# A mean over 8,192 rows: two pairs folded at double width, another engine for one group, and a last piece of one block stored as one row

## The chip, the cores and the metric

The kernel runs on one core of one Trainium2 chip. The metric is the device time of one execution in microseconds (us), and the profile's span, first to last instruction, is some 2 us shorter.

## The reference

```
x = randn(8192, 8192) in fp32
out = mean(x, axis=0)          # 8192 values
```

The input is 268 MB and the output 32 KB. Each input byte is used once.

## The kernel before

The rows form 64 groups of 128, one row for each partition. `bufs` holds six rows of 8,192 columns per partition. Rows 0 to 3 are two buffers, each for a pair of groups (8.39 MB, 64 KB per partition). Row 4 is `both`, a scratch row, and row 5 is `acc`. VectorE folds each pair into `both` and then adds that to `acc`. SyncE issues all loads, each of which waits until VectorE has read the buffer that it overwrites.

```python
add(bufs[:, 2:4, :], bufs[:, 2:4, :], bufs[:, 0:2, :], [first])
add(bufs[:, 4:6, :], bufs[:, 4:6, :], bufs[:, 2:4, :], [second])
add(acc, acc, both, [])
tc.keep_in_program_order(nc.scalar.copy(out=warm[:], in_=ones[:]))
g = 6
while g < G - 10:
    u = (g + 2) % 4
    dma = load_rows(g, u, 2)
    add(both, bufs[:, u, :], bufs[:, u + 1, :], [dma])   # the pair's buffer is free after this
    add(acc, acc, both, [])
    g += 2
# ... single groups 54 to 61 ...
load(r62, rows(g))
tc.keep_in_program_order(nc.gpsimd.tensor_add(
    out=acc[:, 13 * F:], in0=acc[:, 13 * F:], in1=r62[:, 13 * F:]))
g += 1
for lo, hi in [(0, 8), (12, 14), (14, 16)]:              # F = 512 columns
    load(r63[:, lo * F:hi * F], rows(g)[:, lo * F:hi * F])
```

The sum over partitions is made by TensorE with a matrix of 1/M. Each block of columns goes to a group of 32 rows of a PSUM bank, so that a result lies on partitions 0, 32, 64 and 96 and is stored from these four. The end of the kernel copies the banks to SBUF and stores them:

```python
copy(tails[0], ends[0][:])                                # ScalarE
nc.vector.tensor_copy(out=tails[1], in_=ends[1][:])
landed(...)                                               # SyncE waits for earlier loads
s01 = store(nc.sync, ..., res[0:P:32, 0:2, :])            # first eight blocks
s3 = store(nc.scalar, *end(0))                            # blocks 12 and 13
store(nc.sync, *end(1))                                   # blocks 14 and 15, the last piece
landed(loads[-2], s2)
landed(loads[-1], adds[-1])
landed(s01, s3)
```

## Time and profile before

| | before |
|---|---|
| time, median of 3 | 628.64 us (628.49 to 628.82) |
| profiled span | 626.7 us |
| last load lands | 623.02 us |
| from there to the end of the span | 3.69 us |
| share of the DMA engines, 2 to 622 us | 1.00 |

The prediction below shows the page, the stretches and the end of the chain. I call **lead** the time from a load's issue to the landing of the load ahead of it in the queue. While the lead is long, the DMA engines have the next load's work before they finish the last one's. These are the issues of two of the loads in SyncE's timeline (start us, length us, what), and below them pieces of the chain that ended last (start us, length us, what), in which "DMA" is the time from a load's issue to its landing.

```profile
97.94 0.33 SPq L75 DMA_DIRECT2D bufs<-in_x_dram  x1
```

```profile
115.45 27.50 DMA bufs<-in_x_dram
...
345.23 29.93 DMA bufs<-in_x_dram
...
461.35 29.91 DMA bufs<-in_x_dram
```

The load issued at 97.94 follows one that lands at 104.22, a lead of 6.3 us. In the steady part a load takes 29.9 us from issue to landing while loads land every 19.35 us, so the lead there is 29.9 − 19.35 = 10.6 us.

### The profile page before, as it was taken

To read this page: it belongs to the slowest core of one execution; us is meant where nothing else is said; L and a number is where in the kernel's file an instruction comes from. 1 tells how busy PE (TensorE), PEld (TensorE's weight loads), DVE (VectorE), ACT (ScalarE), POOL (GpSimd) and SP (SyncE) were. 2 spreads that over 40 slices of the span, in tenths; PEclk is the share of its full clock that TensorE was granted. 3 is DMA by queue.
4 is the path that set the end of the run, shared out by engine and by line. 5 is a ranking of instruction groups with operands and counts; after the bars stand their busy time and mean duration, and the time that the engine had idled before them with its cause. 6 is when DMAs were issued, how large, how long until landed. Compare 5 with 4: busy or idle time off the path is not lost.

```text
span 626.7 us, 475 instructions
## 1 busy us (share of the span) xinstructions
PE 17.6 (3%) x124; PEld 5.1 (1%) x124; DVE 526.1 (84%) x60; ACT 3.5 (1%) x6; POOL 4.0 (1%) x7
## 2 busy tenths in 40 slices
PE   0000100000000000000000000000000000000027
PEld 0000000000000000000000000000000000000002
DVE  0028999999888998888988889888898888999991
ACT  0000000000000000000000000000000000000001
POOL 0000000000000000000000000000000000000002
PEclk9999999999999999999999999999999999999999
DMA  9999999999999999999999999999999999999997
GB/s 385 468 402 409 461 443 427 410 460 406 464 402 468 402 468 402 468 402 468 402 468 402 468 402 468 402 460 410 443 427 414 456 402 435 435 435 435 420 433 305
DMA packets 5926, 268.50 MB, mean 428 GB/s; under 512 B 656, under 2 KB 664, under 8 KB 1060
## 3 DMA queue, kind: packets, MB, share of 16 engines
q1 hardware_dynamic: 5908, 268.46, 99.2%
q8 instruction: 1, 0.02, 0.0%
q10 hardware_dynamic: 16, 0.01, 0.0%
q14 instruction: 1, 0.01, 0.0%
HBM read 268.44 MB, written 0.03 MB: 428 GB/s over the span
## 4 chain that ended last, share of the span: by engine, by line
DMA 56%; DVE 33%; another core or an unknown queue 10%; issue 0%; SPq 0%; PE 0%; ACTq 0%; POOLq 0%; POOL 0%
DMA bufs<-in_x_dram 56%; DVE bufs L95 33%; SPq L75 0%; PE end L169 0%; ACTq L98 0%; DVE tail L201 0%; POOLq L98 0%; POOL ready L62 0%; POOL ones L59 0%; POOLq L228 0%
## 5 line engine op out<-in xcount | busy, mean ns | idle before, releaser
L95 DVE TENSOR_TENSOR bufs<-bufs 128x8192 f32<-128x8192 f32 (+3 forms) x59 | 525.6, 8909 | 87.9 <-DMA bufs<-in_x_dram 43.8
L169 PE MATMUL bank<-bufs,ones 128*32 128x512 f32 x74 | 12.8, 709 | 540.4 <-DVE bufs L95 539.9
L201 DVE COPY tail<-end 128x256 f32<-128x256 f32 x1 | 0.4, 425 | 10.2 <-PE end L169 10.2
L169 PEld LDWEIGHTS bank<-bufs,ones 128*32 128x32 f32 x74 | 3.2, 120 | 549.5 <-DVE bufs L95 541.6
L136 POOL TENSOR_TENSOR bufs<-bufs 128x1536 f32<-128x1536 f32 x1 | 3.5, 3469 | 614.6 <-DMA bufs<-in_x_dram 614.6
L183 ACT COPY bufs<-bank 128x512 f32<-128x512 f32 x3 | 1.8, 586 | 619.2 <-PE bank L169 616.6
L169 PE MATMUL bank<-ahead,ones 128*32 128x512 f32 x8 | 1.9, 1058 | 65.7 <-DMA ahead<-in_x_dram 65.7
L169 PE MATMUL end<-bufs,ones 128*32 128x256 f32 x36 | 3.3, 384 | 0.1
L169 PE MATMUL bank<-head,ones 128*32 128x512 f32 x6 | 1.9, 600 | 0.0
L169 PEld LDWEIGHTS end<-bufs,ones 128*32 128x32 f32 x36 | 1.4, 109 | 2.4 <-DMA bufs<-in_x_dram 0.9
L116 ACT ACT_TABLE_LOAD x1 | 1.3, 1283 | 0.7 <-PEq L228 0.7
L169 PEld LDWEIGHTS bank<-ahead,ones 128*32 128x32 f32 x8 | 0.2, 140 | 65.6 <-issue 65.6
L183 ACT COPY bufs<-end 128x256 f32<-128x256 f32 x1 | 0.4, 378 | 0.0
L169 PEld LDWEIGHTS bank<-head,ones 128*32 128x32 f32 x6 | 0.4, 108 | 0.6 <-issue 0.6
L116 ACT COPY warm<-ones 128x32 f32<-128x32 f32 x1 | 0.2, 218 | 0.0
L62 POOL TENSOR_TENSOR ready<-ones 128x1 f32<-128x1 f32 x1 | 0.2, 193 | 0.1
L59 POOL MEMSET ones<- 128x32 f32 x1 | 0.1, 125 | 0.3 <-POOLq L228 0.3
L228 POOL MEMSET const-bfloat16-1.0<- 128x1 bf16 x1 | 0.1, 101 | 0.0
L228 POOL MEMSET const-uint8-127<- 128x1 uint8 x1 | 0.1, 101 | 0.0
L228 POOL MEMSET const-float32-0.0<- 128x1 f32 x1 | 0.1, 99 | 0.2 <-issue 0.2
L228 POOL MEMSET const-float32-1.0<- 128x1 f32 x1 | 0.1, 99 | 0.0
## 6 DMA issues: line engine op xcount, KB each, us to landing
bufs<-in_x_dram SPq DMA_DIRECT2D x8, 4096.0 KB, 24.1
bufs<-in_x_dram SPq DMA_DIRECT2D x1, 3328.0 KB
bufs<-in_x_dram SPq DMA_DIRECT2D x1, 2048.0 KB, 20.2
ahead<-in_x_dram SPq DMA_DIRECT2D x1, 1024.0 KB
bufs<-in_x_dram SPq DMA_DIRECT2D x2, 512.0 KB, 21.5
head<-in_x_dram SPq DMA_DIRECT2D x1, 768.0 KB
bufs<-in_x_dram SPq DMA_DIRECT2D x26, 29.9
out_dram<-bufs ACTq DMA_DIRECT2D x1, 8.0 KB
```

The costliest lines, as they stand in the source:

```text
L59: nc.gpsimd.memset(ones[:], 1.0 / M)
L62: nc.gpsimd.tensor_add(out=ready[:], in0=ones[:, 0:1], in1=ones[:, 1:2]))
L95: ins = nc.vector.tensor_add(out=dst, in0=a, in1=b).ins
L116: tc.keep_in_program_order(nc.scalar.copy(out=warm[:], in_=ones[:]))
L136: tc.keep_in_program_order(nc.gpsimd.tensor_add(out=acc[:, 13 * F:], in0=acc[:, 13 * F:], in1=r62[:, 13 * F:]))
L169: tc.keep_in_program_order(nc.tensor.matmul(out=dst[32 * q:32 * q + 32, :], lhsT=ones[:], rhs=cols, start=all(d is not dst or k != q for d ...
L183: tc.keep_in_program_order(nc.scalar.copy(out=dst, in_=src))
L201: nc.vector.tensor_copy(out=tails[1], in_=ends[1][:])
L228: nc = _bacc.Bacc("TRN2", target_bir_lowering=False, num_devices=1)
```

## The change

It has three parts. Pairs 3 and 4 are each added in one instruction of 16,384 columns to `both` and `acc` together, and one fold of `both` into `acc` follows; this saves two instructions on VectorE. Group 62's blocks 12 to 15 go to VectorE; before, GpSimd added three of them and TensorE summed the fourth. The last piece is one block of 512 columns, its two sums of 256 are copied side by side to one partition, and the store is a single row on ScalarE's queue.

```diff
+    for g in (6, 8):
+        u = (g + 2) % 4
+        add(bufs[:, 4:6, :], bufs[:, 4:6, :], bufs[:, u:u + 2, :], [load_rows(g, u, 2)])
     add(acc, acc, both, [])
     tc.keep_in_program_order(nc.scalar.copy(out=warm[:], in_=ones[:]))
-    g = 6
+    g = 10
     while g < G - 10:
 ...
-    load(r62, rows(g))
-    tc.keep_in_program_order(nc.gpsimd.tensor_add(
-        out=acc[:, 13 * F:], in0=acc[:, 13 * F:], in1=r62[:, 13 * F:]))
+    add(acc[:, WHOLE * F:], acc[:, WHOLE * F:], r62[:, WHOLE * F:], [load(r62, rows(g))])
     g += 1
-    for lo, hi in [(0, 8), (12, 14), (14, 16)]:
+    for lo, hi in [(0, 8), (12, 15), (15, 16)]:
 ...   (the plan of sums and the PSUM tiles follow these pieces)
-    copy(tails[0], ends[0][:])
-    nc.vector.tensor_copy(out=tails[1], in_=ends[1][:])
+    nc.vector.tensor_copy(out=tail3, in_=three[:])                 # 384 columns, 4 rows
+    nc.vector.tensor_copy(out=tail1[:, :W], in_=one[0][0:1, :])    # 256 columns, 1 row
+    nc.scalar.copy(out=tail1[:, W:], in_=one[1][32:33, :])
 ...
-    s3 = store(nc.scalar, *end(0))
-    store(nc.sync, *end(1))
+    s3 = store(nc.sync, out[WHOLE * F:15 * F].rearrange("(q c) -> q c", q=4), tail3[0:P:32, :])
+    store(nc.scalar, out[15 * F:].rearrange("(q c) -> q c", q=1), tail1)
```

(The copies are shown without their wrappers. The first add of GpSimd, `ready`, goes too.)

## The prediction

> **What bounds the kernel now.** I read the page first. Its engine row and its slices show what is full from beginning to end.
>
> ```profile
> PE 17.6 (3%) x124; PEld 5.1 (1%) x124; DVE 526.1 (84%) x60; ACT 3.5 (1%) x6; POOL 4.0 (1%) x7
> ...
> DMA  9999999999999999999999999999999999999997
> ...
> HBM read 268.44 MB, written 0.03 MB: 428 GB/s over the span
> ```
>
> The reader is to see that the sixteen DMA engines are busy in every slice but the last, and that VectorE at 84% is not the limit. A table of stretches then leaves out both edges (columns: stretch, its length, busy us of PE, PEld, DVE, ACT, POOL, the clock, the DMA share, GB/s).
>
> ```profile
> 2.00:622.00 620.00, 15.98 (x108) 4.72 (x112) 525.63 (x59) 1.09 (x4) 3.47 (x1) 1.00 1.00 433
> 622.00:627.00 5.00, 1.60 (x24) 0.36 (x15) 0.42 (x1) 1.17 (x3) 0.00 (x0) 0.93 0.11 39
> ```
>
> The DMA share is 1.00 over 620 us. The input has to be read once and is read once, so only two things can move the time: a hole in the stream, or the edges. The head edge is about 2 us and the change does nothing to it (the first load is issued at 0.74 us and waits for no GpSimd work). The tail edge is read from the chain that ended last and from the timeline (start us, length us, what).
>
> ```profile
> 601.09 21.93 DMA bufs<-in_x_dram
> 623.02 0.04 issue
> 623.06 0.68 PE end L169 x8
> 623.75 0.03 issue
> 623.77 0.42 DVE tail L201
> ```
>
> ```profile
> 623.20 0.70 SPq L186 DMA_DIRECT2D out_dram<-bufs  x1
> 623.48 0.52 ACTq L186 DMA_DIRECT2D out_dram<-bufs  x1
> ...
> 624.22 0.56 SPq L186 DMA_DIRECT2D out_dram<-tail  x1
> ```
>
> The last load lands at 623.02. Then come 0.73 us until the sums of the last piece stand in PSUM, 0.45 us of copy, 0.56 us of issue (until 624.78), and 1.93 us of store, receipt and closing barrier until 626.71. That is a tail of 3.69 us. It is 0.6% of the span, so even its half would be 0.3%.
>
> **What the Trainium skill says.** "DMA: Bandwidth & Descriptors", Specifications, gives a fabric ceiling of 435 GB/s; the trace agrees with 433 GB/s between 2 and 622 us, so the stream has nothing left. The same page, "Anatomy of one DMA", puts most of a DMA's fixed cost of about 2 us into the write receipt and not into the data; here 1.93 us lie after the last issue for 4 KB, though that includes the closing barrier. Its section "Why a DMA increments its semaphore by 16 and not by 1" lets a transfer of one row use one engine where one of four rows uses four; the packet records before show four completion packets for the last store, which agrees for four. "VectorE: DVE Perf Modes", the errata section, has (N+151)/0.96 ns for an fp32 add: 8,691 ns for 8,192 columns and 17,224 for 16,384. The groups by form show 8,692 and 17,225, so it may be used for the new add of 2,048: 2,291 ns.
>
> **The change, part by part.**
>
> Pairs 3 and 4 at double width. Before, each costs 8,692 + 8,692 ns on VectorE (fold the pair into one row, add the row to the accumulator). Now it is one 17,225 ns add, and one more fold of 8,692 follows the two, in place of the one ahead of them. That saves 2 x 0.16 us of an engine that is not the bound: worth nothing. The cost is in buffer release: the loaded pair was free after the first 8.7 us, now only after 17.2. The chain gives the landings: the load issued at 115.45 lands 27.50 later, at 142.96, and pairs land every 19.35 us (8.39 MB at 433 GB/s), so those before it land at 123.6, 104.2 and 84.9. VectorE is now free from 80.4 on, so the add for the pair landing at 84.9 runs from 84.95 to 102.2, and the next load is issued there instead of at 97.94. The load ahead of it in the queue lands at 104.2: the lead shrinks from 6.3 to 2.0 us. The following one: 104.3 + 17.2 = 121.5 against a landing at 123.6, lead 2.1 us (before: issue at 115.45, 8.1 us). Afterwards the old scheme wins back 1.9 us per pair. The very first load took 1.0 us from issue (0.74) to its first packet (1.74 in the packet records), and a landing is posted some 0.5 us after its last data packet (622.53 and 623.02 at the end). So 2.0 - 1.0 - 0.5 leaves about 0.5 us before the stream would have a hole. Estimate: 0, with a chance of one in five of 0.1 to 0.5 us.
>
> Group 62 on VectorE. Out goes GpSimd's add of 1,536 columns (3.47 us, from 615.74 to 619.22, for which TensorE waited 0.4 us); in comes a VectorE add of 2,048 columns, 2.29 us, on an engine idle since 613.54: done near 618.0. TensorE's queue is then still in the rows up to 618.29. It finishes this stage earlier, but then waits for the load landing at 620.47: worth nothing.
>
> The last piece. The 2 x 512 KB become 768 KB and 256 KB. Per engine and partition the packets of 4 KB took 0.160 us; those of 2 KB took 0.084 and of 6 KB 0.234 elsewhere, and 8 x (0.234 + 0.084) = 2.54 against 16 x 0.160 = 2.56, so the last landing stays at 623.02. The 768 KB piece lands 8 x 0.084 = 0.67 us earlier, at 622.35, just when TensorE comes free (622.32). Its four sums of 384 columns end near 623.27, and VectorE copies them (425 + 128 / 0.96 = 558 ns) from 623.29 to 623.85. The last block's two sums of 256 columns start at 623.06 as before and stand at 623.74 (four became two, 0.01 earlier). ScalarE copies one half (378 ns) by 624.15; VectorE must first finish the other copy, so its half ends at 623.87 + 0.42 = 624.29 against 624.20 before: **+0.09**.
>
> The last store is now one row. Loads, whose rows are neighbouring partitions, take 328 ns to issue (median of 38); the stores that gather every 32nd partition take 515 to 1,071. I take a single row for the cheap kind: 0.33 against 0.56: **-0.23**. One completion in place of four, which were posted over 0.08 us: **-0.05**.
>
> The closing waits. The other tail store, of the 384-column sums, is issued at about 623.95 behind the 0.70 us issue of the first eight blocks, ends issuing at 624.5, and should land 1.05 us after that as the last one did before (624.78 to 625.87), at 625.55. SyncE then still works through some 0.3 us of waits, until about 625.87, which is where the last wait ended before. So of 0.09 - 0.23 - 0.05 = -0.19 us I expect only a small part, about 0.05, to reach the end.
>
> Out of GpSimd's `ready` add (0.19 us at 0.94 us, nothing on the path): 0.
>
> Sum: 628.64 - 0.05 = 628.59, rounded to 628.6 us.
>
> **The rivals.** First, a hole in the stream: if a load issued 2 us ahead is too late, the engines stand still twice and each hole goes into the time whole. The ScalarE store that took 1.9 us from issue (620.57) to its first packet (622.50) speaks for it, but it queued behind loads; the estimate of 1.0 us speaks against. It would make 628.8 to 629.5. Second, the tail gains fully, because the 384-column store isn't in the way: 628.64 - 0.19 = 628.45; with the two VectorE copies overlapping, 628.35. Third, the two stores, issued 0.4 us apart on two queues, get in each other's way: before, ScalarE's store issued until 623.99 sent its first packet 0.86 us later, SyncE's alone 0.64; with that, 628.8.
>
> **Range and chances.** The three times before differ by 0.33 us. The gains reach down to 628.3, a hole and the stores' conflict up to 629.2; with half of the noise on either side I take 628.0 to 629.3. Two per cent are 12.6 us. The whole tail is 3.7 us, so faster by that much can't be had, and slower would need a stall of twenty times the margin that I computed.
>
> **What would show it right or wrong.** The DMA share stays 1.00 between 2 and 622 us and the chain's last load lands at 623.0; a landing at 623.2 or later is the hole. The load issues stand near 102.2 and 121.5 us. VectorE's add of 2,048 columns takes 2.29 us from 615.65. Its two last copies end near 623.85 and 624.29. The last ScalarE issue takes 0.33 us; 0.5 would refute that step. The span ends about 3.6 us after the last landing. The prediction is wrong if the single row costs a full issue, if the double-width adds starve the stream, or if another execution differs from this one by more than the parts I sum.

## The result, and the profile after

The changed kernel took **631.45 us** (median of six, 631.21 to 631.57) against 628.73 (628.49 to 628.96) for six runs of the kernel before on the same chip. The ratio is 1.0043, with a 95% interval of 1.003 to 1.0056. A ratio is the mean time of one kernel's fast runs over that of the other's in the same rounds, so it is not quite the ratio of the medians. This is 2.7 us slower and lies outside my range.

The page of the changed kernel, its engine row and its slices, and then the stretch that leaves out both edges (columns as in the prediction):

```profile
PE 16.9 (3%) x112; PEld 4.3 (1%) x112; DVE 528.5 (84%) x60; ACT 3.6 (1%) x6; POOL 0.3 (0%) x5
...
DMA  9999999999999999999999999999999999999996
...
HBM read 268.44 MB, written 0.03 MB: 426 GB/s over the span
```

```profile
2.00:622.00 620.00, 13.48 (x84) 3.43 (x84) 527.60 (x58) 2.08 (x3) 0.00 (x0) 1.00 1.00 432
```

These views look untouched: a 9 in every slice but the last, a share of 1.00, and 432 GB/s in place of 433. The share is an average of sixteen engines over 620 us, and 2 us on the slowest engine are too small for it. The chain shows them, because its pieces end at landings:

```profile
80.39 23.81 DMA bufs<-in_x_dram
...
104.26 17.24 DVE bufs L92
...
121.52 8.70 DVE bufs L92
...
156.55 27.73 DMA bufs<-in_x_dram
...
603.00 20.26 DMA bufs<-in_x_dram
```

The load issued at 80.39 still lands at 104.20, as before. The double-width add runs from 104.26 to 121.50, in the place of two adds with a buffer release between them. The piece of 27.73 us ends at 184.28, where before the same load landed at 181.65. The last piece of the chain shown ends at 623.26 with the landing of the last group's first eight blocks; before, these landed at 620.47, 2.8 us earlier. SyncE's timeline has the two loads that were to be issued late:

```profile
102.16 0.33 SPq L72 DMA_DIRECT2D bufs<-in_x_dram  x1
```

```profile
121.51 0.33 SPq L72 DMA_DIRECT2D bufs<-in_x_dram  x1
```

Every landing is counted by sixteen semaphore events, one from each DMA engine. From the trace's events, the last of the sixteen and the time from the first to the last of them ("spread"):

| load | before: issue, lands, spread | after: issue, lands, spread |
|---|---|---|
| pair at 80.4 | 80.42, 104.22, 0.38 | 80.39, 104.20, 0.54 |
| first late one | 97.94, 123.58, 0.40 | 102.16, **125.34, 2.23** |
| second late one | 115.45, 142.96, 0.40 | 121.51, **145.56, 2.19** |
| next | lands 162.28, 0.37 | lands 164.92, 2.21 |
| last of all | lands 623.02 | lands 625.74 |

The delay is 1.76 us at the first late load, 2.60 at the second, and stays there: the last landing is 2.72 us later. The spread stays too, at 2.0 to 2.2 us to the end. Every engine carries eight 64 KB packets of every load (8 × 2.42 us make the 19.35 us between landings), so an engine that has fallen behind here is not relieved. The median engine lost only 1.3 us; the end waits for the slowest.

In the packet records around the first late load, every engine's packets of the kernel before follow each other without a gap (one ends at 103.45 and the next starts at 103.46, and so on). The changed kernel has a gap:

```
                                     before              after (issue at 102.16)
last packet of the old load ends     103.45 to 103.80    103.24 to 103.77
first packet of the new one starts   103.46 to 103.80    103.24 to 104.85
length of that packet (64 KB)        2.42                2.42 to 3.23
engines busy, every 0.25 us from 103.25:
  before   16 16 16 16 16 16 16 16
  after    16 11  9  8 10 13 15 16
```

The new load's first packet starts 1.1 us after its issue on the first engine, which had been busy with the old load until then, and **2.7 us after it on the last**.

The other part of the loss is at the end. This is the timeline of the changed kernel after its last landing at 625.74:

```profile
625.99 0.71 SPq L183 DMA_DIRECT2D out_dram<-bufs  x1
626.08 0.56 DVE L194 COPY head<-end 128x384 f32<-128x384 f32 x1 [5.36 <-PE end L166]
626.51 0.36 ACT L196 COPY head<-end 1x256 f32<-1x256 f32 x1 [0.54 <-PE end L166]
626.56 0.40 DVE L195 COPY head<-end 1x256 f32<-1x256 f32 x1
626.80 0.56 SPq L183 DMA_DIRECT2D out_dram<-head  x1
627.04 0.25 ACTq L183 DMA_DIRECT2D out_dram<-head  x1
```

The single row costs 0.25 us of issue, and its one packet starts at 627.76. But the store of the 384-column sums is issued at 626.80 and sends its packets at 628.04 to 628.18; SyncE gets past it at 628.53 and then works through four more waits until 628.89. Before, the last wait ended 2.86 us after the last landing (625.88), now 3.16 us after. The last receipt of a store is no later than before (2.78 us after the landing, before 2.85); the waits left behind it are what is new. The tail is 629.71 − 625.74 = 3.97 us in place of 3.69.

### The profile page after: what moved, and what is told of

It is laid out like the page before. It is cut to its first block, busy times and chain, and to the rows that moved or that the text cites. A ratio compares the mean times of both kernels' runs of the same rounds, so it can differ in the third digit from the quotient of the medians.

```text
span 629.7 us, 447 instructions
## 1 busy us (share of the span) xinstructions
PE 16.9 (3%) x112; PEld 4.3 (1%) x112; DVE 528.5 (84%) x60; ACT 3.6 (1%) x6; POOL 0.3 (0%) x5
## 4 chain that ended last, share of the span: by engine, by line
DMA 54%; DVE 35%; another core or an unknown queue 10%; PE 0%; issue 0%; ACTq 0%; POOL 0%; POOLq 0%
DMA bufs<-in_x_dram 54%; DVE bufs L92 34%; PE bank L166 0%; PE end L166 0%; ACTq L95 0%; DVE head L194 0%; DVE head L195 0%; POOL ones L59 0%; POOLq L95 0%; POOLq L225 0%
## 5 line engine op out<-in xcount | busy, mean ns | idle before, releaser
L92 DVE TENSOR_TENSOR bufs<-bufs 128x8192 f32<-128x8192 f32 (+4 forms) x58 | 527.6, 9097 | 93.1 <-DMA bufs<-in_x_dram 43.7
L166 PE MATMUL end<-bufs,ones 128*32 128x384 f32 (+1 forms) x24 | 2.5, 454 | 0.0
L116 ACT ACT_TABLE_LOAD x1 | 1.3, 1283 | 104.3 <-DMA bufs<-in_x_dram 104.3
## 6 DMA issues: line engine op xcount, KB each, us to landing
bufs<-in_x_dram SPq DMA_DIRECT2D x26, 29.9
```

Source lines behind the costliest of these rows:

```text
L92: ins = nc.vector.tensor_add(out=dst, in0=a, in1=b).ins
L166: tc.keep_in_program_order(nc.tensor.matmul(out=dst[32 * q:32 * q + 32, :], lhsT=ones[:], rhs=cols, start=all(d is not dst or k != q for d ...
```

## The experiments

Every kernel here gave a correct result. "Before" is the kernel before on the same chip in the same rounds. Since the changed kernel differs from it in three parts, I first took these apart (the first four runs share one set of runs of the kernel before), then made a late load by itself, then looked at VectorE's program length, which the first runs brought up, and last at the tail.

**no_double**: the changed kernel with pairs 3 and 4 as before.

```diff
-    for g in (6, 8):
-        u = (g + 2) % 4
-        add(bufs[:, 4:6, :], bufs[:, 4:6, :], bufs[:, u:u + 2, :], [load_rows(g, u, 2)])
-    g = 10
+    g = 6
```

> The changed kernel with pairs 3 and 4 folded at single width again; its tail stays. Theory (late buffer release: the loads issued only 2.0 us ahead leave the stream a hole): the last landing returns to 623.0 us, the landing spread of the sixteen engines to under 0.6 us, and what stays over the kernel before is the tail's 0.3 us, so 629.0 us. Rival (the tail change is what costs): 631 us. Rival (ScalarE's table load, which the double-width code also pushes from 0.7 to 104 us): 629.0 too, this run does not tell it apart.

Measured: 629.38 (629.32 to 630.16) against 628.57; ratio 1.0015 (1.0001 to 1.0028). About 0.8 us of the 2.7 stay, more than I had expected; the rest went away with the double width, which is thus the larger part. The landings are undelayed until 485 us (spread 0.61) and then 0.5 us late with a spread of 1.15. At that point the packet records hold one packet of 8 KB of an instruction queue, from 485.54 for 0.325 us, beside which a 64 KB packet took 3.08 us in place of 2.42. The page lists the queue, but in the same words for the kernel before, where that packet lies outside the stream of loads. These are the page's lines of the instruction queues of the kernel before (packets, MB, share):

```profile
q8 instruction: 1, 0.02, 0.0%
...
q14 instruction: 1, 0.01, 0.0%
```

Its tail was 3.98 us, as long as the changed kernel's.

**early_warm**: the double-width adds also moved ScalarE's first copy, and with it a 1.28 us table load, from 0.7 to 104.3 us, right into the hole. This rival is taken away by putting the copy ahead of the two adds.

```diff
+    tc.keep_in_program_order(nc.scalar.copy(out=warm[:], in_=ones[:]))
     for g in (6, 8):
 ...
-    tc.keep_in_program_order(nc.scalar.copy(out=warm[:], in_=ones[:]))
```

> The changed kernel, with ScalarE's warm-up copy put ahead of the double-width pairs, so that its table load runs at 0.7 us again and not at 104.3 us, in the middle of the hole. Late-release theory: no change, 631.4 us. Table-load rival: 629.0 us.

Measured: 631.47 (631.15 to 631.9); ratio 1.0045 (1.0033 to 1.0058). Nothing came back, and the load issued at 102.12 landed at 125.89. The table load isn't the cause.

**double_only**: the kernel before with the double-width adds alone.

```diff
+    for g in (6, 8):
+        u = (g + 2) % 4
+        add(bufs[:, 4:6, :], bufs[:, 4:6, :], bufs[:, u:u + 2, :], [load_rows(g, u, 2)])
-    g = 6
+    g = 10
```

> The kernel before, with only pairs 3 and 4 at double width. Late-release theory: 628.7 + 2.7 = 631.4 us, with loads issued at 102.2 and 121.5 us and the last landing at 625.7. If the tail change caused the loss: 628.7 us.

Measured: 631.08 (630.76 to 631.53) against 628.57; ratio 1.004 (1.0028 to 1.0053). This part alone costs 2.5 us. The profiled run was the fastest of its set (630.76), and its last landing was 624.87, 1.85 us late. The late load, issued at 102.38, landed at 124.73, 1.15 us behind. The second one, issued with a lead of 3.0 us, lost nothing more. Another 0.7 us went to loads that landed between 183 and 242 us, although they were issued 6.7 to 10.9 us ahead; in the packet records 64 KB packets take up to 2.70 us there in place of 2.42, and at most one engine at a time stands idle, for 0.6 us in all. Nor is all of the 2.5 us in the stream: the tail is 4.01 us with the stores and receipts of the kernel before, because VectorE's last step of the closing barrier ends 3.80 us after the last landing in place of 3.27. The cause of both is open.

**late_warm**: the kernel before with the table load alone moved to the third pair.

```diff
-    tc.keep_in_program_order(nc.scalar.copy(out=warm[:], in_=ones[:]))
 ...
+        if g == 10:
+            tc.keep_in_program_order(nc.scalar.copy(out=warm[:], in_=ones[:]))
```

> The kernel before, with only ScalarE's warm-up copy moved behind the pairs 3 and 4, so that its table load falls past 100 us. Late-release theory: 628.7 us. Table-load rival: 631 us.

Measured: 628.59 (628.46 to 628.92) against 628.57; ratio 1.0. This closes the rival from the other side.

**late_one**: the kernel before, in which one load of the steady part also waits for the fold into `acc`, so that it is issued late. No instruction of VectorE changes.

```diff
+    late = []                                  # load() also waits for what is in it
 ...
+        if g == 34:
+            late.append(adds[-3])
         dma = load_rows(g, u, 2)
```

> The kernel before, same instructions, but one load in the steady middle (pair 34, near 325 us) waits also for the accumulate add, so it is issued 1.9 us ahead of the landing before it instead of 10.6. Late-release theory: that load lands 1 to 2.3 us late, the landing spread of the engines jumps from 0.3 to 1 or 2 us and stays there to the end, the time is 629.8 to 630.9 us. Rival (the loss comes from what VectorE does in a double-width add, not from when the load is issued): 628.6 us.

Measured: 629.71 (629.59 to 630.34) against 628.63; ratio 1.0019 (1.0007 to 1.0032). SyncE's timeline shows the issue, first in the kernel before and then in this one, and the chain the cost (start us, length us, what):

```profile
325.88 0.33 SPq L75 DMA_DIRECT2D bufs<-in_x_dram  x1
```

```profile
334.51 0.33 SPq L77 DMA_DIRECT2D bufs<-in_x_dram  x1
```

```profile
306.45 29.90 DMA bufs<-in_x_dram
...
345.13 30.76 DMA bufs<-in_x_dram
...
384.67 29.93 DMA bufs<-in_x_dram
```

The late load was issued at 334.51 where the kernel before has it at 325.88, with a lead of 1.84 us in place of 10.6, and landed at 356.55, 0.8 us late. The load behind it, issued on time at 345.13, took 30.76 us in place of 29.93: it inherits the delay. After that, nearly all loads take 29.9 us again, but none wins the 0.8 us back; the spread went from 0.47 to 0.79 us and stayed. The last landing was 624.02 (before: 623.02): two later loads, landing at 511.5 and 597.2 us, lost another 0.14 and 0.13 us with leads of 10.6 and 14.4, for which I have no cause. The packets repeat the picture of the changed kernel: the first packets start 1.0 to 2.0 us after the issue, and take up to 3.24 us. So the lateness of one load makes a hole, with no double-width add, and no other part of the change, in the kernel.

**late_all**: the same for all twenty loads of pairs 14 to 52.

```diff
-        if g == 34:
+        if g >= 14:
             late.append(adds[-3])
```

> As the run with one late load, but all twenty loads of pairs 14 to 52 wait for the accumulate add, each with 1.9 us of lead. If every late load costs again: 628.6 plus 20 times 0.5 to 2 us, 640 to 670 us. If only the first costs, since later the fast engines wait at each load for the slowest and it loses nothing more: 630 to 632 us.

Measured: 653.33 (652.77 to 657.15) against 628.63; ratio 1.0409. That is 24.7 us, or 24.7 / 20 = 1.24 us for each late load. The holes add up, but unevenly. By the landings, seven of the loads lost 2.4 to 3.5 us each, one lost 1.4 and twelve at most 0.5. The seven had leads of 1.8 to 2.2 us, but four others with 2.0 to 2.4 lost at most 0.4. A load behind one that landed late often had more (eight had 3.1 to 5.3 us), so this is not the run with 1.9 us for each that I had expected. The spread also fell back, from 3.37 to 0.67 us for one, when the engines that were ahead lost time too.

**late_3**: as late_one, but the fold is cut at column 6,900 and the load waits only for the part ahead of the cut, so that the lead is 3.2 us.

```diff
+        if g == 34:
+            late.append(adds[-4])
 ...
+        if g == 30:
+            add(acc[:, :6900], acc[:, :6900], both[:, :6900], [])
+            add(acc[:, 6900:], acc[:, 6900:], both[:, 6900:], [])
+        else:
+            add(acc, acc, both, [])
```

> As the run with one late load, but the accumulate add ahead is cut at column 6900 and the load waits for its first part only: a lead of 3.2 us. If the last of the engines gets its first packet 2.7 us after the issue, as the trace of the changed kernel shows, and landings are posted 0.5 us late, 3.2 us is just enough: no hole or one below 0.5 us, 628.6 to 629.1 us. VectorE has one instruction more; if that alone brings an instruction fetch into the stream, it shows as an 8 KB packet of the instruction queue in the middle and costs 0.5 us more.

Measured: 629.79 (629.56 to 630.15) against 628.63; ratio 1.002 (1.0005 to 1.0035). At a lead of 3.19 us the load landed 0.4 us late, half as much as at 1.84, and the spread went from 0.29 to 0.68. The total is no smaller than late_one's, because this kernel has a second event: its VectorE program has one instruction more, and the 8 KB instruction packet appeared in it at 476.31 us, after which the spread was 1.26. So the run is a clean measure of the landing only, not of the time. A lead of 3.2 us isn't enough here; 4.5 us (the kernel before, at 61.02 and 80.42) and 6.3 us (at 97.94, and no_double at 97.97) are.

**plus2**: the second event by itself. The kernel before, with two adds of one column on VectorE while it is idle at 613 us.

```diff
+    scr = sb.tile([P, 2], f32, name="scr")
+    for j in range(2):
+        tc.keep_in_program_order(nc.vector.tensor_add(out=scr[:, j:j + 1], in0=ones[:, 0:1], in1=ones[:, 1:2]))
```

> The kernel before, with two adds of one column on VectorE while it is idle near 613 us, so that its program is as long as that of the changed kernel at single width. Theory of the instruction fetch (that run had an 8 KB instruction packet at 485.5 us, beside which one engine fell 0.54 us behind for good): the same packet appears and the time is 629.1 us. Rival (the 0.8 us of that run lie all in the tail): 628.6 us.

Measured: 629.28 (629.02 to 629.55) against 628.63; ratio 1.0011 (0.9998 to 1.0023). The interval just includes 1, but all five runs lie above all nine of the kernel before (628.41 to 628.82), and the landings show the loss. The work added comes 130 us after the place where the time is lost. In the chain:

```profile
422.54 29.93 DMA bufs<-in_x_dram
...
461.25 30.51 DMA bufs<-in_x_dram
...
500.53 29.92 DMA bufs<-in_x_dram
...
601.57 21.93 DMA bufs<-in_x_dram
```

The load issued at 461.25 takes 30.51 us (29.91 before). The 8 KB packet of the instruction queue ran at 485.47 for 0.325 us, the spread went from 0.54 to 1.11 us, and the last load landed at 623.50. Counted in the built programs, VectorE has 71 instructions in the kernel before, the changed kernel, early_warm and the other late ones, and 69 in double_only: none of these has the packet in mid-stream. It has 72 in late_3 and 73 in no_double and plus2, and all three have it, each time when 47 of VectorE's instructions in the trace have started. So the changed kernel's double width saved two instructions that its own add and copy then used up; without it the fetch of some 0.5 us comes instead. The double width thus avoided a loss of about 0.5 us and made one of some 2.2 (double_only without its barrier) to 2.7 us.

**tail71**: the changed kernel's tail at single width with 71 instructions on VectorE. TensorE sums group 62's four blocks, and ScalarE copies the 384-column sums.

```diff
-    add(acc[:, WHOLE * F:], acc[:, WHOLE * F:], r62[:, WHOLE * F:], [load(r62, rows(g))])
+    load(r62, rows(g))
 ...
+        (r62, 12, 15),
+        (r62, 15, 16),
 ...
-        nc.vector.tensor_copy(out=tail3, in_=three[:]).ins,
+        tc.keep_in_program_order(nc.scalar.copy(out=tail3, in_=three[:])).ins,
```

> The changed kernel's last pieces and stores at single width, with VectorE's program kept as short as in the kernel before: group 62's four blocks are summed by TensorE instead of a VectorE add, and ScalarE copies the 384-column sums. Theory: no 8 KB instruction packet in the stream, last landing at 623.0 us, and a tail of 3.9 us behind it (3.98 in the two traces with these stores), because SyncE waits for the 384-column store, issued behind the 0.70 us issue of the first eight blocks: 628.7 to 628.9 us. If the single-row store decides the tail: 3.4 us and 628.3.

Measured: 630.85 (629.72 to 631.14) against 628.64; ratio 1.0029. The runs fall into two groups, two at 629.7 and three at 630.8 to 631.1, and the profiled one is of the first. My expectation failed. There was no 8 KB packet, but the other instruction queue's one packet, of 16 KB and 1.08 us, ran at 620.59, amid the last pieces, and their spread went from 0.59 to 1.72 us. In the kernel before it ran at 622.36 and in no_double at 622.21, when nearly all data was through. That it belongs to TensorE is only argued. TensorE's built program is longer than that of the changed kernel (262 instructions against 238) but not than that of the kernel before (262 too); what differs from that one is that 48 of the 62 sums, in place of 46, stand ahead of the last group's loads. The tail of this run is 3.71 us, shorter than the 3.9 I had expected.

**cand**: tail71 with the first eight blocks stored in two pieces, so that the final wait for the 384-column store comes last.

```diff
-    s01 = store(nc.sync, ..., res[0:P:32, 0:2, :])
+    s0, s1 = [store(nc.sync, ..., res[0:P:32, b, :]) for b in range(2)]
 ...
-    landed(s01, s3)
+    landed(s0, s1)
```

> As the run before it, with two more edits: the first eight blocks are stored in two pieces, the first as soon as bank 0 is copied, so that the 384-column store is issued some 0.15 to 0.25 us earlier, and SyncE waits for that store last and not ahead of 0.3 us of other waits. Theory (that store and the waits behind it set the end): a tail of 3.4 to 3.6 us and 628.3 to 628.5 us, just below the kernel before at 628.6. If something else sets it: as the run before it.

Measured: 630.32 (630.2 to 630.53) against 628.64; ratio 1.0027. It misses for the same reason (the 16 KB packet at 620.27, the last landing at 624.31); its median is 0.5 us below that of tail71, but its five runs lie between tail71's two groups, so this shows no gain. In its profile the tail is 4.15 us: one of the four completions of the 384-column store came at 627.53, 0.75 us after the other three. Why is open.

**tail_only**: GpSimd keeps most of group 62's blocks (1,280 columns) and TensorE takes 768, so that neither program grows past that of the kernel before.

```diff
+    mid = WHOLE * F + 2 * V                    # V = 384
+    tc.keep_in_program_order(nc.gpsimd.tensor_add(
+        out=acc[:, mid:], in0=acc[:, mid:], in1=r62[:, mid:]))
 ...
-        (r62, 12, 15),
-        (r62, 15, 16),
+        (r62, 12, 13.5),
```

> The changed kernel's last pieces and stores, at single width, with VectorE's program as short as before, and now with fewer sums on TensorE ahead of the last loads than in the run tail71, where a 16 KB packet of the instruction queue ran at 620.6 us and one engine's last pieces came 1.1 us late. Theory: no 8 KB packet in the middle, the 16 KB one at 622 us or later as in the kernel before, last landing at 623.0 us, tail 3.8 to 4.0 us behind it since the 384-column store waits behind the 0.7 us issue: 628.7 to 628.9 us. If the time of the 16 KB packet depends on nothing that I moved: 629.7 again.

Measured: 628.88 (628.63 to 628.97) against 628.63; ratio 1.0003 (0.999 to 1.0015). The 16 KB packet is back at 622.06, the last landing at 623.13. What is left is the tail, 3.93 us against 3.69. It accounts for the 0.25 us between the medians, which by themselves are not clear of noise. Its timeline:

```profile
623.36 0.71 SPq L187 DMA_DIRECT2D out_dram<-bufs  x1
...
624.17 0.56 SPq L187 DMA_DIRECT2D out_dram<-head  x1
624.36 0.25 ACTq L187 DMA_DIRECT2D out_dram<-head  x1
```

**cand2**: tail_only with the stores and waits of cand.

```diff
-    s01 = store(nc.sync, ..., res[0:P:32, 0:2, :])
+    s0, s1 = [store(nc.sync, ..., res[0:P:32, b, :]) for b in range(2)]
 ...
-    landed(s01, s3)
+    landed(s0, s1)
```

> As tail_only, with the first eight blocks stored in two pieces and SyncE waiting for the 384-column store last. Theory (that store's issue and the waits behind it set the end): a tail of 3.3 to 3.6 us and 628.2 to 628.5 us, a little below the kernel before at 628.6. Rival (the last load decides and the order of stores and waits is hidden): the same as tail_only.

Measured: **628.27** (628.07 to 628.34) against 628.63 (628.55 to 628.91); ratio 0.9993 (0.9979 to 1.0007). All five runs lie below all ten of the kernel before, though the interval doesn't exclude 1, so I call it a probable gain of 0.3 us and no more. Its timeline:

```profile
622.40 1.37 SPq L187 DMA_DIRECT2D out_dram<-bufs  x2
...
623.89 0.50 SPq L187 DMA_DIRECT2D out_dram<-head  x1
624.28 0.25 ACTq L187 DMA_DIRECT2D out_dram<-head  x1
```

The first of the two stores of eight blocks no longer waits for the second bank, so SyncE's queue is free when the 384-column sums are copied: that store goes at 623.89 in place of 624.17. Two waits are left behind it, the last ending at 625.65 in place of 626.23. The tail is 3.45 us, 3.69 − 3.45 = 0.24 us shorter than in the kernel before. No run separates the one-row store's share of that from the share of the new order of stores and waits.

## Why the prediction was wrong

**What bounds the kernel: right.** The stream of loads is the bound, and as I wrote, only a hole in it or the edges can move the time. Both did.

**When the loads are issued: right.** I had 102.2 and 121.5 us, and measured 102.16 and 121.51. VectorE's double-width add delays a release by one add of 8.7 us, and the idle time ahead of it gives half of that back.

**Whether that makes a hole: wrong, and this is the step that failed.** It reads: "So 2.0 - 1.0 - 0.5 leaves about 0.5 us before the stream would have a hole. Estimate: 0". The terms of 2.0 and 0.5 hold (a lead of 2.04; 0.43 us from the last data packet at 103.77 to the landing at 104.20). The term of 1.0 is the mistake. I took the first packet of the first load of the program, at 1.74 us, when the memory was idle and only one of sixteen engines had to start. Even there the sixteen engines' first packets start between 1.74 and 2.45 us, so up to 1.7 us after the issue. Under load it was 1.1 us for the first engine and 2.7 for the last. The page "DMA: Bandwidth & Descriptors" of the Trainium skill has, in "Latency and other measured facts", an access latency of HBM of 0.2 us on average and 2 us at high load; read with care, it would have warned that an idle start says little about a start in the full stream. The 1.1 to 2.7 us agree with it in size, but no run shows that it is the memory that takes this time.

Two more terms were missing from the sum. The first packets after a gap take 2.42 to 3.23 us in place of 2.42. And I thought of a hole as time lost by all engines alike, at most 0.5 us, while the end is set by the slowest engine: by the end the median engine had lost 1.3 us and the slowest one 2.7.

The parts account for the loss, though less exactly than they seem to. The double width alone costs 2.5 us (double_only) and the tail alone 0.25 (tail_only), which makes 2.75; the changed kernel lost 631.45 − 628.73 = 2.72. But some 0.3 us of double_only's loss lies in its closing barrier, and tail_only's tail is not quite that of the changed kernel. In the two profiles the loss is 2.72 us at the last landing and 0.28 us in the tail. That the lead is the cause, and not the width of the add or the table load, is shown by late_one, late_all, early_warm and late_warm. The kernel before agrees: its own double-width add at 63.17 ran beside a load that landed on time (84.88) and had been issued 4.5 us ahead, at 61.02. My first rival was this one, with 628.8 to 629.5 and one chance in five. (The store named for it sent its first packet at 622.37, not at 622.50, so 1.8 us after its issue.) Even one late load costs 0.8 us at its landing and 1.1 us of time (late_one), and the change makes two.

**Group 62 on VectorE: right.** The add took 2.29 us, starting at 618.43 (615.65 plus the delay of the stream), and cost nothing by itself. What I hadn't thought of is its instruction, and that of the extra copy, in VectorE's program: without the two that the double width saved they would have cost 0.5 us (no_double, plus2).

**The last piece: right.** The four sums' copy took 0.56 us (predicted 558 ns), the single row 0.25 us to issue (predicted 0.33 and the cheap kind); in the packet records it is one packet with one completion. The two copies ended 0.90 and 1.22 us after the last landing, where I had 0.83 and 1.27. The two VectorE copies overlapped by 0.08 us.

**The closing waits: right mechanism, wrong size.** I named the 384-column store and the waits behind it as the thing that hides the gain, and put them at −0.05 us; they came to about +0.28 (3.97 against 3.69; the timed tail_only has +0.25). I had the last wait end where it ended before, 2.86 us after the last landing. It ended at 3.16: the store was issued 0.13 us later than I had it (1.06 after the landing in place of 0.93), its receipt came 1.17 us after its issue ended in place of 1.05 (the times given with that figure, 624.78 and 625.87, make 1.09), and the waits behind it took 0.36 us in place of 0.3. cand2 shows that these were what hid the gain.

**What stays open.** At nearly the same lead the hole differed: 0.8 us in late_one, 1.15 in double_only, 1.76 in the changed kernel and, with landing at 125.89, 2.3 in early_warm. I don't know what decides which engine starts late and by how much. Nor is it settled why the second late load of the changed kernel lost another 0.84 us with a lead of 3.83 us, when early_warm's lost 0.14 with 4.42 and double_only's nothing with 3.01. The lead is measured at the last engine's landing, and with a spread of 2.2 us it says too much for the others: in the packet records one engine had finished the load ahead at about 122.8, only 1.3 us after this load's issue at 121.51. It then stands idle until 125.07, 3.5 us after the issue, and why so long is unknown. Open too are the later losses of double_only and its barrier. That the instruction packet comes between 71 and 72 instructions is known from these programs alone, and what in a program places it is not.

## What to carry to other kernels

In a kernel bound by its loads, a buffer's release has to come so early that the next load is issued well before the load ahead of it lands: here 4.5 us were enough in a stream that ran evenly, 3 to 4 us lost between nothing and 0.8 us, about 2 us lost 0.8 to 2.3 at a first late load, and nothing lost came back. So don't save work on an engine with idle time by an instruction that holds a loaded buffer longer. When a change of the end of a program moves the time by half a microsecond, look at the landings in the middle for a packet of instructions, and at the waits in the order in which the last engine works through them, before giving the difference to the change itself.

## What the Trainium skill lacked or had wrong

- "DMA: Bandwidth & Descriptors" gives a latency of about 0.6 us to the first byte for a load issued from SyncE, and HBM's 2 us under load in another row. It lacks what the two make for a transfer over sixteen engines: a load of 8.39 MB issued when the queue was nearly empty started on its first engine after 1.1 us and on its last after 2.7, and its first 64 KB packets took up to 3.23 us in place of 2.42.
- The same page says that the engines finish independently, but not that an engine that falls behind stays behind while every load has the same share for each and is issued in time: the spread of 2.0 to 2.2 us lasted from 125 to 625 us, with the slowest engine 2.7 us late and the median one 1.3.
- "Runtime: NRT & Kernel Launch", "Instruction fetch mechanics", has the instructions fetched in blocks of 16 KiB while the program runs, and calls the cost of crossing a block's boundary mostly hidden. It lacks what such a packet costs a program that keeps every DMA engine busy. In these runs one of 8 KB for 0.325 us came in mid-stream when VectorE's program had 72 or 73 instructions and not with 71, and put one engine some 0.55 us behind for good (about 0.65 us of time in plus2); one of 16 KB took 1.0 to 1.4 us near the end, and widened the spread by 1.1 us when it came at 620.59 in place of 622.36.
- No page that I read has the cost of issuing a store by its partitions: a single row took 0.25 us to issue, four rows on every 32nd partition 0.50 to 0.65 us, and 1.07 to 1.09 for ScalarE's store of four blocks.
